# Four low parts of split weights trade places between VectorE and the adding DMA

## The chip, the cores and the metric

The kernel runs on one core of one Trainium2 chip. The metric is the device time of one execution in microseconds (us), taken as the median of several executions. A core has TensorE (PE in the profile; PEld is its weight load), VectorE (DVE), ScalarE (ACT), GpSimd (POOL), SyncE (SP), and 16 DMA engines that every queue shares.

## The reference

One decoder layer on 256 tokens with a model width of 1024, in float32, batch 1 and depth 1. Per layer it computes:

```
h = rms_norm(x, norm1_g);  proj = h @ w_in            # 1024 x 2560
attn = block-sparse attention on 8 heads of 64 (256 tokens: one causal block)
conv = silu(layer_norm(causal depthwise conv, 31 taps, of GLU))
x = x + concat(attn, conv) @ w_out                    # 1024 x 1024
h = rms_norm(x, norm2_g)
y = x + (silu(h @ w_gate) * (h @ w_up)) @ w_down      # 1024 x 2816, twice, and 2816 x 1024
```

The change touches only how the weights of the last line are prepared.

## The kernel before

**Two parts of every weight.** To keep float32 accuracy, the kernel splits each weight into a high part `wh` (the weight rounded to the form that TensorE multiplies fast) and a low part `wl` (the weight minus `wh`). Each product is then two or three matmuls: `wh` and `wl` against the activation, and `wh` against the activation's own low part. Weights are handled in pieces of 128 x 1024, numbered from 0. A high part is always made by ScalarE (line 278). A low part is made in one of two ways, in `low_part`:

- by VectorE: one subtraction, line 226;
- by adding DMA: ScalarE writes -`wh` into the place of `wl` (line 223), and a DMA that GpSimd issues adds the weight to it while it moves it (line 224). The weight comes from device memory for most pieces ("wl<-w" in the profile), or from a tile on chip where the piece is not stored as such ("wl<-t").

The list `BY_DMA` (line 65) names the pieces of the second kind.

**The order.** Nothing schedules at run time: the Python program writes the instructions of all engines in one fixed order, and every engine works through its own list in that order. Before each group of matmuls, `feed` (line 274) makes the high parts of the pieces up to some pieces ahead, and the low parts of those that are nearly due. `BEHIND` lists pieces whose high part is made some places earlier than their number says. Eight places hold pieces; a new piece takes the place of the lowest numbered one and so waits until TensorE is through with that.

**The stages around the change.** Pieces 28 to 71 are the gate and up weights: the loop over `f` from 0 to 21 (the lines of `mm2`, 307 and 309, tiles `fg` and `fu`) uses piece 28 + 2f for the gate and 29 + 2f for the up half, 16 pairs of matmuls in each `f`. After each `f`, `glu_task` evacuates the two banks with ScalarE (`gs`, `us`, line 314) and VectorE (`tg`, `ps`, `ac`, lines 315, 857, 871) and a Silu on ScalarE (line 859). Pieces 72 to 102 are the down projection, 11 pairs of weight blocks (line 953, tile `sum`). Nine of the pairs are "FAST": a Strassen-like scheme that forms seven products from sums of weight blocks. For such a pair VectorE makes the sums (`add_up`, lines 241 to 243, tile `t`), and the pair has three pieces: the first is the block as stored, the second and third are sums in `t`. Piece 72, 73 and 74 are those of pair 0, and 75, 76, 77 those of pair 1. Beside these three each FAST pair has a single block (`b11` or `other`, lines 207 and 208). At the end VectorE, and ScalarE with GpSimd, add the seven sums onto the residual (lines 1003 to 1020), and SyncE writes the result out.

Of the kernel before, what the change touches and what calls it, by code (L numbers as in the profile page):

```python
# [61 lines left out]
PLAIN = [p for p in range(NF // 2) if PAIRS[p] == "P"]  # L62
DOWN = 72
BEHIND = {75: 70, 78: 72, 81: 75, 82: 78, 83: 78, 86: 80, 89: 83, 92: 86, 95: 89, 98: 92}
BY_DMA = [*range(45, 64, 3), 73, 74, *BEHIND]
FAR = 46
SUMS = {66: 0, 69: 1}
FORMS_LATE = 11
# [72 lines left out]
def _build(nc, tc, t, ctx):  # L141
# [78 lines left out]
    def low_part(dst, src, by_dma=False):  # L220

        if by_dma:
            nc.scalar.activation(dst[1], dst[0].bitcast(F32), AF.Copy, scale=-1.0)  # L223
            nc.gpsimd.dma_start(dst[1], src.bitcast(F32R), accum_op=ALU.add)  # L224
        else:
            nc.vector.tensor_tensor(dst[1], src, dst[0].bitcast(F32), op=ALU.subtract)  # L226
# [27 lines left out]
    def home(j):  # L254

        i, a = divmod(j * PIECE, BW)
        if j >= DOWN:
            p, a = down[j - DOWN]
            if a and p in FAST:
                return None  # L260
            i, a = DOWN // 2 + p, (a if p in PLAIN else 1) * PIECE
        return t["w"][i - 2][:, a:a + PIECE]
# [11 lines left out]
    def feed(upto, more=1):  # L274
        last = DOWN + len(down) - 1
        while len(pieces) <= min(upto + more, last):
            dst, src, j = new_piece()
            nc.scalar.activation(dst[0], src, AF.Copy)  # L278
            if j in BY_DMA:
                low_part(dst, home(j) or src, True)  # L280
            waiting.append((dst, src, j))
            waiting.sort(key=lambda w: w[2])
        while waiting and waiting[0][2] <= upto:
            dst, src, j = waiting.pop(0)
            if j not in BY_DMA:
                low_part(dst, src)
# [802 lines left out]
```

## Time and profile before

| what | value |
|---|---|
| median of 3 runs | 286.4 us (286.2 to 286.47) |
| the profiled execution's own time | 287.12 us |
| its span, first to last instruction | 285.3 us |
| TensorE clock granted in it | 0.999 |
| PE busy | 279.6 us |
| DVE busy | 238.9 us |
| ACT busy | 207.2 us |
| POOL busy | 46.9 us |
| DMA moved | 69.03 MB |

The span lies 1.8 us under the profiled execution's own time, and that execution 0.7 us above the median of the runs; sums in the prediction are made against the profiled execution. An instruction's row in a timeline reads: start, duration, engine, line, operation, tile written <- tiles read, shapes, count, and in brackets how long its engine sat idle before it and what ended that. The printed end of one instruction may lie some 0.1 us behind the start of the next on the same engine, since they are pipelined. Share of busy time over the whole span is an average over stages; the tables by stage show what each stage is limited by.

### The profile page before, as it was taken

How to read it: one execution, taken by the hardware profiler on the slowest of the kernel's cores; microseconds unless marked ns; L12 is line 12 of the kernel's file. 1: busy time of each engine (PE TensorE's matmuls, PEld its weight loads, DVE VectorE, ACT ScalarE, POOL GpSimd, SP SyncE). 2: the span in 40 equal slices, each digit the busy share in tenths (PEclk: the TensorE clock that was granted, in tenths of full speed). 3: DMA queues.
4: the chain of work that ended last, by engine and by line, in shares of the span. 5: the costliest groups of instructions: out<-in, count | busy, mean ns of one | idle time of the engine just before them, and what ended most of it. 6: DMA issues, size and time to landing. Idle time of an engine off the chain costs nothing.

```text
span 285.3 us, 4176 instructions
## 1 busy us (share of the span) xinstructions
PE 279.6 (98%) x1463; PEld 234.1 (82%) x1463; DVE 238.9 (84%) x425; ACT 207.2 (73%) x336; POOL 46.9 (16%) x75
## 2 busy tenths in 40 slices
PE   8899999999999999999999999999999999999994
PEld 6688887778788888888888888888888878888883
DVE  3979996896894959999967687698789789999995
ACT  4858578986728677467878777776679799887480
POOL 0003555533000000000111111000012221211033
PEclk9999999999999999999999999999999999999999
DMA  7999958854203882849689998984676999999603
GB/s 228 409 423 341 420 188 275 314 177 177 119 0 148 319 308 110 295 149 369 229 273 289 300 324 227 288 273 167 231 223 153 247 270 255 316 318 194 170 14 147
DMA packets 13638, 69.03 MB, mean 242 GB/s; under 512 B 1777, under 2 KB 2385, under 8 KB 7730
## 3 DMA queue, kind: packets, MB, share of 16 engines
q1 hardware_dynamic: 10162, 56.19, 53.5%
q0 software_dynamic: 3312, 12.58, 21.5%
q8 instruction: 11, 0.18, 0.2%
q14 instruction: 9, 0.07, 0.1%
q10 hardware_dynamic: 144, 0.00, 0.0%
HBM read 65.62 MB, written 2.10 MB: 237 GB/s over the span
## 4 chain that ended last, share of the span: by engine, by line
PE 87%; DMA 6%; DVE 4%; issue 1%; POOL 0%; SPq 0%; ACT 0%; POOLq 0%
PE p L724 19%; PE sum L953 17%; PE fg L307 12%; PE fu L307 12%; PE po L770 8%; PE fg L309 6%; PE fu L309 6%; DMA wl<-t 4%; DMA first<-first 2%; PE S L558 1%; PE pT L588 1%; DVE wl L226 1%; PE O L744 1%; PE xT L786 1%; PE cv L318 0%
## 5 line engine op out<-in xcount | busy, mean ns | idle before, releaser
L278 ACT ACTIVATE wh<-raw 128x1024 fp32r<-128x1024 f32 x81 | 83.9, 1054 | 15.4 <-PE fu L307 7.5
L226 DVE TENSOR_TENSOR wl<-raw,wh 128x1024 fp32r<-128x1024 f32 x64 | 77.1, 1219 | 3.4 <-ACT wh L278 3.4
L307 PE MATMUL fu<-g,wh 128*128 128x512 f32 x176 | 62.5, 395 | 0.0
L307 PE MATMUL fg<-g,wh 128*128 128x512 f32 x176 | 62.4, 394 | 0.0
L309 PE MATMUL fg<-g,wl 128*128 128x256 f32 x176 | 48.8, 277 | 0.0
L309 PE MATMUL fu<-g,wl 128*128 128x256 f32 x176 | 48.8, 277 | 0.0
L307 PEld LDWEIGHTS fg<-g,wh 128*128 128x128 f32 x176 | 33.0, 187 | 7.7 <-DVE g L794 0.2
L307 PEld LDWEIGHTS fu<-g,wh 128*128 128x128 f32 x176 | 33.0, 188 | 7.6
L224 POOL DMA_DIRECT2D wl<-w x17 | 14.9, 877 | 133.2 <-ACT wl L223 61.8
L309 PEld LDWEIGHTS fg<-g,wl 128*128 128x128 f32 x176 | 33.1, 188 | 0.0
L309 PEld LDWEIGHTS fu<-g,wl 128*128 128x128 f32 x176 | 33.1, 188 | 0.0
L953 PE MATMUL sum<-wh,forms 128*128 128x512 f32 x96 | 29.5, 389 | 0.0
L724 PE MATMUL p<-wh,xh 128*128 128x512 f32 x80 | 25.9, 405 | 0.8 <-ACT wh L385 0.8
L278 ACT ACTIVATE wh<-t 128x1024 fp32r<-128x1024 f32 x18 | 19.1, 1059 | 8.0 <-DVE t L241 4.9
L724 PE MATMUL p<-wh,xl 128*128 128x512 f32 x80 | 24.8, 391 | 0.0
L724 PE MATMUL p<-wl,xh 128*128 128x512 f32 x80 | 24.7, 390 | 0.0
L953 PEld LDWEIGHTS sum<-wh,forms 128*128 128x128 f32 x96 | 18.0, 188 | 3.7
L223 ACT ACTIVATE wl<-wh 128x1024 fp32r<-128x1024 f32 x19 | 20.2, 1062 | 0.6
L226 DVE TENSOR_TENSOR wl<-t,wh 128x1024 fp32r<-128x1024 f32 x16 | 19.6, 1223 | 1.2 <-ACT wh L278 0.8
L953 PE MATMUL sum<-wl,forms 128*128 128x512 f32 x48 | 18.8, 391 | 0.3 <-DMA wl<-t 0.3
L724 PEld LDWEIGHTS p<-wh,xh 128*128 128x128 f32 x80 | 14.2, 189 | 5.3 <-ACT wh L385 1.6
L724 PEld LDWEIGHTS p<-wh,xl 128*128 128x128 f32 x80 | 15.0, 188 | 3.3
(208 smaller groups left out, 476.6 us busy)
## 6 DMA issues: line engine op xcount, KB each, us to landing
raw<-w SPq DMA_DIRECT2D x44, 1024.0 KB, 6.6
wl<-w POOLq DMA_DIRECT2D x17, 512.0 KB, 9.3
first<-first SPq DMA_DIRECT2D x8, 384.0 KB, 7.0
raw<-w SPq DMA_DIRECT2D x2, 512.0 KB, 7.5
xtok<-xtok SPq DMA_DIRECT2D x2, 512.0 KB, 8.8
x<-xtok SPq DMA_DIRECT2D x2, 512.0 KB, 6.7
kept<-x POOLq DMA_DIRECT2D x1, 1024.0 KB, 4.1
wl<-t POOLq DMA_DIRECT2D x2, 512.0 KB, 9.5
```

What stands on the lines that cost most here:

```text
L223: nc.scalar.activation(dst[1], dst[0].bitcast(F32), AF.Copy, scale=-1.0)
L224: nc.gpsimd.dma_start(dst[1], src.bitcast(F32R), accum_op=ALU.add)
L226: nc.vector.tensor_tensor(dst[1], src, dst[0].bitcast(F32), op=ALU.subtract)
L278: nc.scalar.activation(dst[0], src, AF.Copy)
L307: nc.tensor.matmul(out.rearrange("p (a q) -> p a q", a=2), w[0], both, start=z in first and z not in seen, stop=False)
L309: nc.tensor.matmul(out[:, 0:T], w[1], both[:, 0, :], start=False, stop=z in last and left[z] == 0)
L558: nc.tensor.matmul(banks[a][:, out], G["qT"][rows, j, q], G["kT"][rows, j, k], start=True, stop=True)
L588: nc.tensor.transpose(b[:, a * P:(a + 1) * P], p[:, a * P:(a + 1) * P], ident)
L724: nc.tensor.matmul(banks[i], (xh, xh, xl)[a][:, kt, sls[i]], w[a % 2], start=kt == 0 and a == 0, stop=kt == KT - 1 and a == 1)
L744: nc.tensor.matmul(o, vs[:, 0, hs], G["pT"][h][:, 0:T], start=True, stop=False)
L770: nc.tensor.matmul(po[i, n], G["mix"][l][:, k, i * P:(i + 1) * P], w[r], start=k == a == 0, stop=k == KT - 1 and a == 2)
L953: nc.tensor.matmul(banks[m], lhs, rhs, start=first, stop=last)
```

## The change

```diff
-BY_DMA = [*range(45, 64, 3), 73, 74, *BEHIND]
+BY_DMA = [*range(45, 72, 3), *BEHIND]
```

Before, the list held 45, 48, ... 63, then 73 and 74, and the ten of `BEHIND`. Now it holds 45, 48, ... 63, 66, 69 and the ten of `BEHIND`. So the low parts of pieces 66 and 69 (the gate weights of f = 19 and the up weights of f = 20) go from VectorE to the adding DMA, and those of 73 and 74 (the two sums of pair 0 of the down projection) from the adding DMA to VectorE. Instructions stay the same in number on every engine; no matmul changes. The order in which high parts are made, and the places that they take, stay as they are.

GpSimd's queue, where the adding DMAs are issued, as a difference (- before, + now):

```order
 L224 DMA wl60_1951<-w 128x1024
 L224 DMA wl63_2040<-w 128x1024
-L224 DMA wl75_2273<-w 128x1024
-L224 DMA wl78_2366<-w 128x1024
-L224 DMA wl73_2398<-t0_2340 128x1024
-L224 DMA wl74_2424<-t0_2340 128x1024
+L224 DMA wl66_2128<-w 128x1024
+L224 DMA wl69_2219<-w 128x1024
+L224 DMA wl75_2275<-w 128x1024
+L224 DMA wl78_2368<-w 128x1024
 L224 DMA wl81_2456<-w 128x1024
 L224 DMA wl82_2541<-w 128x1024
```

The two from the tile `t0` behind piece 78 are gone; two from device memory stand ahead of piece 75.

VectorE's list at the end of the gate and up loop (f = 19 and 20), where pair 0 and pair 1 of the down projection are prepared. Before:

```order
L208 TENSOR_TENSOR b11l_1081<-raw36_2072,b11h_1080 128x512
L315 TENSOR_TENSOR ps8_2344<-fu19_2334,us19_2403 128x256
L871 TENSOR_TENSOR ps8_2344<-ps8_2344,tg19_2370 128x256
L241 TENSOR_TENSOR t1_2428<-raw37_2131 128x1024
L242 TENSOR_TENSOR t1_2428<-t1_2428,raw37_2131 128x512
L243 TENSOR_TENSOR t1_2428<-t1_2428,raw37_2131 128x512
L315 TENSOR_TENSOR tg20_2432<-fg20_2395,gs20_2433 128x256
```

The same place now:

```order
L208 TENSOR_TENSOR b11l_1081<-raw36_2072,b11h_1080 128x512
L226 TENSOR_TENSOR wl73_2400<-t0_2342,wh73_2399 128x1024
L315 TENSOR_TENSOR ps8_2346<-fu19_2336,us19_2404 128x256
L871 TENSOR_TENSOR ps8_2346<-ps8_2346,tg19_2372 128x256
L226 TENSOR_TENSOR wl74_2425<-t0_2342,wh74_2424 128x1024
L241 TENSOR_TENSOR t1_2428<-raw37_2133 128x1024
L242 TENSOR_TENSOR t1_2428<-t1_2428,raw37_2133 128x512
L243 TENSOR_TENSOR t1_2428<-t1_2428,raw37_2133 128x512
L315 TENSOR_TENSOR tg20_2432<-fg20_2397,gs20_2433 128x256
```

Two subtractions of 128 x 1024 stand ahead of the sums `t1` of pair 1 and ahead of the evacuation of f = 20.

ScalarE's list at the same place. Before:

```order
L207 ACTIVATE b11h_1080<-raw36_2072 128x512
L278 ACTIVATE wh73_2397<-t0_2340 128x1024
L223 ACTIVATE wl73_2398<-wh73_2397 128x1024
L859 ACTIVATE tg19_2370<-tg19_2370 128x256
L314 ACTIVATE us19_2403<-fu19_2334 128x256
L278 ACTIVATE wh74_2423<-t0_2340 128x1024
L223 ACTIVATE wl74_2424<-wh74_2423 128x1024
L314 ACTIVATE gs20_2433<-fg20_2395 128x256
```

The same place now:

```order
L207 ACTIVATE b11h_1080<-raw36_2072 128x512
L278 ACTIVATE wh73_2399<-t0_2342 128x1024
L859 ACTIVATE tg19_2372<-tg19_2372 128x256
L314 ACTIVATE us19_2404<-fu19_2336 128x256
L278 ACTIVATE wh74_2424<-t0_2342 128x1024
L314 ACTIVATE gs20_2433<-fg20_2397 128x256
L278 ACTIVATE wh81_2455<-raw39_2249 128x1024
L223 ACTIVATE wl81_2456<-wh81_2455 128x1024
L859 ACTIVATE tg20_2432<-tg20_2432 128x256
L314 ACTIVATE us20_2462<-fu20_2398 128x256
L278 ACTIVATE wh76_2482<-t1_2428 128x1024
```

The two copies of line 223 are gone here, and stand directly behind `wh66` and `wh69`, earlier in the loop over `f`. What follows on ScalarE (`wh81`, `wl81`, the Silu of `tg20`, `us20`, `wh76`) is the same in both.

## The prediction

> **What bounds the kernel now.** I read the page first, then who keeps TensorE waiting, then busy time by stage, then the timelines of VectorE and ScalarE where the edit acts.
>
> ```profile
> span 285.3 us, 4176 instructions
> PE 279.6 (98%) x1463; PEld 234.1 (82%) x1463; DVE 238.9 (84%) x425; ACT 207.2 (73%) x336; POOL 46.9 (16%) x75
> ```
>
> Over the whole span TensorE looks like the only bound. Its waits, with the chain of waits around the one that touches the edit:
>
> ```profile
> PE sum L953 <- DMA wl<-t: 0.3, 1, 0.3
> 231.26 0.50 PE L953 MATMUL sum<-wl,forms 128*128 128x512 f32 x1 [0.29 <-DMA wl<-t]
> 221.17 10.05 DMA wl<-t
> 231.26 48.80 PE sum L953 x214
> ```
>
> The one stall behind the start is 0.29 us, at the first use of `wl74`, the second transfer of the kind that the change removes. Nothing more than that can be won on TensorE here. But the average hides a stage:
>
> ```profile
> core 0: us, PE busy (x) PEld busy (x) DVE busy (x) ACT busy (x) POOL busy (x), PEclk, DMA share, GB/s
> 217.00:227.00 10.00, 10.00 (x60) 8.74 (x59) 8.11 (x16) 8.42 (x14) 2.63 (x3) 1.00 0.99 220
> 227.00:240.00 13.00, 12.71 (x57) 10.20 (x56) 11.23 (x18) 12.60 (x18) 2.63 (x3) 1.00 1.03 247
> 240.00:250.00 10.00, 10.00 (x46) 8.27 (x45) 9.81 (x12) 8.59 (x9) 1.75 (x2) 1.00 1.04 319
> 250.00:260.00 10.00, 10.00 (x46) 8.29 (x45) 9.76 (x12) 8.40 (x10) 1.75 (x2) 1.00 1.05 290
> 260.00:270.00 10.00, 10.00 (x46) 8.29 (x45) 9.79 (x11) 5.42 (x7) 0.88 (x1) 1.00 0.76 156
> ```
>
> From 240 us on VectorE is as full as TensorE: 9.8 of 10 us in each stretch, the rest being gaps of hundredths between dependent steps. Who ends last is seen at the very end:
>
> ```profile
> 273.13 2.35 DVE L226 TENSOR_TENSOR wl<-raw,wh 128x1024 fp32r<-128x1024 f32 x2
> 275.41 0.69 DVE L1018 TENSOR_TENSOR rest<-sum,rest 128x512 f32<-128x512 f32 x1
> 276.75 4.31 DVE L1003 SCALAR_TENSOR_TENSOR raw<-sum,rstd,raw 128x512 f32<-128x512 f32 x6
> 280.97 0.47 DVE L1003 SCALAR_TENSOR_TENSOR raw<-sumleft,rstd,raw 128x256 f32<-128x256 f32 x1
> 281.53 0.48 DVE L1003 SCALAR_TENSOR_TENSOR raw<-sumright,rstd,raw 128x256 f32<-128x256 f32 x1
> 277.00 3.81 POOL L1008 TENSOR_TENSOR raw<-raw,rest 128x512 f32<-128x512 f32 x3 [0.36 <-ACT rest L1007]
> 276.96 0.39 PE L953 MATMUL sum<-wl,act 128*128 128x512 f32 x1
> ```
>
> VectorE runs back to back from its last low part (275.48) to 281.44, and the last addition, at 281.53, waits for TensorE. So VectorE reaches the end 0.09 us, or with the 0.08 us by which its instructions overlap 0.17 us, ahead of TensorE. **The kernel is bound by both**, and VectorE has 0.17 us to spare. GpSimd's three additions hang on VectorE's L1018 through ScalarE, so they give no slack of their own.
>
> The Trainium skill (Perfetto Trace Analysis, Identifying the Most-Contended Engine) takes the engine of the highest occupancy for the bottleneck. By that, work put on VectorE at 84% of the span would cost nothing, and the time would follow TensorE's stall; that result is the first rival. The same page says under Optimization Strategy that the most-contended engine may change over time; the stretches from 240 us agree, with VectorE at 98% there.
>
> **The change part by part.**
>
> *Low parts 66 and 69 by adding DMA.* ScalarE gains two copies of 1.06 us, at 192.0 and 200.4, right behind the high parts:
>
> ```profile
> 190.98 1.06 ACT L278 ACTIVATE wh<-raw 128x1024 fp32r<-128x1024 f32 x1 [0.64 <-PE fg L307]
> 193.76 1.06 ACT L278 ACTIVATE wh<-raw 128x1024 fp32r<-128x1024 f32 x1 [1.44 <-PE fu L307]
> 199.30 1.06 ACT L278 ACTIVATE wh<-raw 128x1024 fp32r<-128x1024 f32 x1 [0.51 <-PE fu L307]
> 202.08 1.06 ACT L278 ACTIVATE wh<-raw 128x1024 fp32r<-128x1024 f32 x1 [0.92 <-PE fg L307]
> 207.61 0.42 DVE L315 TENSOR_TENSOR ps<-fu,us 128x256 f32<-128x256 f32 x1 [2.15 <-PE fg L307]
> DMA to landing us min/median/max: 5.5/9.3/11.7
> 224.18 0.40 PE L307 MATMUL fu<-g,wh 128*128 128x512 f32 x1
> 224.53 0.39 PE L307 MATMUL fu<-g,wh 128*128 128x512 f32 x1
> ```
>
> The first copy fits into 1.44 us of idle time, the second overfills 0.92 by 0.1 us, which the next idle time takes. The transfers start near 193 and 201.5; at the slowest landing of any adding DMA (11.7) they are there by 205 and 213. The two matmul rows open the up half of f = 21: a pair takes 0.35 us, an `f` of 16 pairs 5.55, so the up half of f = 20 starts at 218.63 and f = 19 near 210.3: over 5 us to spare each. Cost nothing, hidden by that; a late transfer would cost its lateness. VectorE loses 2 x 1.14 us there and wins nothing, since at 207.61 it waits 2.15 us for f = 17 anyway.
>
> *Low parts 73 and 74 by VectorE.* The wait of 0.29 us on TensorE goes, and VectorE gets two subtractions in front of its full stretch. What they displace:
>
> ```profile
> 217.84 0.68 DVE L208 TENSOR_TENSOR b11l<-raw,b11h 128x512 fp32r<-128x512 f32 x1
> 218.82 0.42 DVE L315 TENSOR_TENSOR ps<-fu,us 128x256 f32<-128x256 f32 x1 [0.30 <-ACT us L314]
> 219.62 1.22 DVE L241 TENSOR_TENSOR t<-raw 128x1024 f32<-128x1024 f32 x1
> 222.66 0.42 DVE L857 TENSOR_TENSOR tg<-tg,r_bc 128x256 f32<-128x256 f32 x1
> 224.25 0.42 DVE L315 TENSOR_TENSOR ac<-fu,us 128x256 f32<-128x256 f32 x1 [1.17 <-PE fg L307]
> 225.36 1.22 DVE L226 TENSOR_TENSOR wl<-t,wh 128x1024 fp32r<-128x1024 f32 x1 [0.22 <-ACT wh L278]
> 226.50 0.42 DVE L878 TENSOR_TENSOR act<-ac,act 128x256 fp32r<-128x256 f32 x1
> 232.62 1.22 DVE L241 TENSOR_TENSOR t<-raw 128x1024 f32<-128x1024 f32 x1
> 239.04 0.69 DVE L208 TENSOR_TENSOR b11l<-raw,b11h 128x512 fp32r<-128x512 f32 x1 [0.34 <-ACT b11h L207]
> 222.58 1.06 ACT L223 ACTIVATE wl<-wh 128x1024 fp32r<-128x1024 f32 x1
> 223.55 0.40 ACT L859 ACTIVATE tg<-tg 128x256 f32<-128x256 f32 x1
> 224.26 1.06 ACT L278 ACTIVATE wh<-t 128x1024 fp32r<-128x1024 f32 x1
> ```
>
> An independent 1024-wide subtraction holds VectorE for 1.14 us (225.36 to 226.50); an engine starts 0.04 us after the end of what it waits for (`wh76`, 224.26 + 1.06, and 225.36). With these steps:
>
> - `wl73` starts at 218.44, the 0.68 of L208 less the overlap of 0.08 behind 217.84, and ends its hold at 219.58, where the evacuation `ps` starts (218.82 before: 0.76 late; the idle 0.30 us is used up). `wl74` starts at 220.38, once `ps` and L871 are through (`wh74`, which waits for TensorE to leave the gate of f = 20 at 218.63, is there by 219.8). The sums of pair 1 start at 221.52 instead of 219.62: 1.90 late, and L857 ends at 224.98 instead of 223.08.
> - Now ScalarE waits. Its Silu of `tg20`, behind `wl81` (over at 223.55), starts at 225.02 instead of 223.55; it and `us20` hold ScalarE 0.60 us, then `wh76` starts at 225.62 instead of 224.26, when TensorE's place let it: 1.36 late. The two copies that ScalarE lost gain nothing, for it waits for this.
> - VectorE's `ac` waits for `us20`: 225.73 (1.48 late; 0.42 of its idle 1.17 is taken up). `wl76` waits for `wh76`: 226.72, 1.36 late. From here each engine waits for the other through f = 21, so their idle times go with the lateness rather than soaking it up: the Silu of `tg21` 1.37 late, `wh77` 1.36, the sums of pair 2 at 233.99 instead of 232.62, `b11l` at 240.36 instead of 239.04, 1.32 late.
> - Behind that VectorE has no idle time left, so 1.32 us reach the tail.
>
> *Next late.* TensorE, 0.29 us earlier now, needs the last low part at 276.67 and gets it at 275.48 + 1.32 + 0.04 = 276.84: it stalls about 0.17 us, most of the gain. Then VectorE's own chain decides: 1.32 late less 0.17 to spare.
>
> *Sum.* 0 (66, 69) - 0 (TensorE's stall, not at the end any more) + 1.32 - 0.17 = **+1.15 us** on 287.12, so 288.27 for the profiled execution, and from the median of 286.4, 287.55. I say 287.5. No operation in this sum is without a row, so the bounds come from the lateness: none of it reaches the tail, and the stall of 0.29 is won (-0.29), or all of 2 x 1.14 = 2.28 does, less 0.17 (+2.11). I take the middle value since each of its steps is set by a row, and the same steps with the old list give back the old starts to 0.05 us.
>
> **The rivals.**
>
> 1. *TensorE alone decides.* The 2.28 us on VectorE are soaked up and the stall at `wl74` goes: 286.4 - 0.3 = 286.1. For it: by the stretches above VectorE idles 1.89 us from 217 to 227 and 1.77 to 240, more than 2.28 in all. Against it: each of these waits ends on ScalarE, which itself waits for VectorE. It holds if less than 0.17 us is left at 240; that makes it no change, and not slower.
> 2. *All of it arrives.* If ScalarE's later `wh` of pair 2 push VectorE once more, up to 2.28 us come through and TensorE stalls at each last low part: 286.4 + 2.1 = 288.5. Against it: ScalarE has two copies less to do in this stage.
> 3. *Transfers come late.* The two new ones, or block loads beside them, miss their use. The DMA engines have room there:
>
> ```profile
> 194.00:198.00 4.00, 4.00 (x25) 3.52 (x24) 3.08 (x7) 2.86 (x6) 0.00 (x0) 1.00 0.62 254
> ```
>
>    `wl66` would need over 17 us to land against the 11.7 seen; each us past that adds one to the forecast, 288.5 at 18 us.
> 4. *The relief helps.* The two transfers gone at 218 leave a share of 0.99 to 1.03 lighter, so loads land earlier. But no engine waits for a load there, so at best rival 1.
>
> **How the numbers follow.** Forecast 0.78, rival 1 with 4 0.13, rival 2 0.07, rival 3 0.02. The forecast's own range is 287.1 to 288.0 (lateness 0.9 to 1.8). A range of 8 in 10 that leaves out most of rivals 1 and 2: 286.6 to 288.1. A measurement of this kernel tells about 0.2%, 0.57 us, from no change: slower 0.82 (forecast, 2, 3, and less a small part of the forecast that falls under 287.0), same 0.14, faster 0.04, since no row offers more than 0.3 us.
>
> **What would show it.** Right: `wl73` and `wl74` on VectorE near 218.4 and 220.4; the idle time before `ac` of f = 20 shrunk from 1.17 to some 0.7; sums of pair 2 near 234; L1018 near 276.7; TensorE's wait on "wl<-t" gone and a short one on VectorE's `wl` near 276.7; the last addition waiting for VectorE itself or GpSimd, not TensorE. Wrong: VectorE's sums of pair 2 at 232.6 (rival 1); a TensorE wait on DMA near 210 or 218 (rival 3); L1018 past 277.3 (rival 2).

## The result, and the profile after

The changed kernel takes 288.07 us (median of 6 runs, 287.83 to 288.88) against 286.44 us for the kernel before on the same chip (6 runs, 286.20 to 287.01). The ratio is 1.0057, with a 95% interval of 1.0047 to 1.0067: **slower by 1.63 us** (1.35 to 1.92). Its profiled execution took 288.44 us.

The head of its page, and its chain of waits by engine:

```profile
span 286.3 us, 4175 instructions
PE 280.5 (98%) x1463; PEld 235.5 (82%) x1463; DVE 239.0 (83%) x425; ACT 207.3 (72%) x336; POOL 46.8 (16%) x75
PE 82%; DVE 9%; ACT 3%; issue 3%; POOL 0%; DVEq 0%; ACTq 0%
```

The same chain in the kernel before:

```profile
PE 87%; DMA 6%; DVE 4%; issue 1%; POOL 0%; SPq 0%; ACT 0%; POOLq 0%
```

Busy time has hardly changed on any engine (VectorE 238.9 before, 239.0 now). What has changed is the chain. The share of DMA is gone, that of TensorE has fallen, and VectorE's has doubled. The chain of the changed kernel in the down projection (start, duration, what), its beginning, a piece from the middle and one near the end, shows where:

```profile
226.86 9.57 PE sum L953 x42
...
239.54 0.53 ACT b11h L207
240.09 0.69 DVE b11l L208
240.78 1.07 DVE other L894 x2
241.85 1.15 DVE t L241
...
275.32 1.22 DVE wl L226
276.54 0.61 DVE rest L1018
```

Behind 236.43 us TensorE is not in it any more: VectorE and ScalarE take turns, and at the end GpSimd has a piece. Before, one row of TensorE, "231.26 48.80 PE sum L953 x214", reached from 231.26 to 280.06.

Busy time by stage of the changed kernel, at the edit and in the first full stretch behind it:

```profile
core 0: us, PE busy (x) PEld busy (x) DVE busy (x) ACT busy (x) POOL busy (x), PEclk, DMA share, GB/s
217.00:227.00 10.00, 10.00 (x60) 8.81 (x59) 8.98 (x15) 6.41 (x12) 0.88 (x1) 1.00 0.70 178
240.00:250.00 10.00, 10.00 (x46) 8.29 (x45) 9.72 (x13) 8.73 (x11) 2.45 (x3) 1.00 1.04 317
```

Where the edit acts, from 217 to 227, VectorE has gone from 8.11 to 8.98 us, ScalarE from 8.42 to 6.41, and the DMA share from 0.99 to 0.70. VectorE had 1.89 us free there before, and 0.87 of them are used now, for 2.28 us of added work; the rest of the 2.28 shows as work that now stands behind 227. From 240 on it is as full as it was (9.72 us, before 9.81).

The two executions did not reach this place at the same moment. In what follows, a time marked **"after the mark"** counts from the first matmul of the down projection in the one profiled execution of each kernel. TensorE works without a gap up to there in both (10.00 us of 10 from 217 to 227), so the change does not delay it:

```profile
226.95 0.62 PE L953 MATMUL sum<-wh,forms 128*128 128x512 f32 x2
```

That is the kernel before; this is the changed one, 0.26 us earlier:

```profile
226.69 0.63 PE L953 MATMUL sum<-wh,forms 128*128 128x512 f32 x2
```

VectorE's timeline of the changed kernel at the edit:

```profile
218.18 1.22 DVE L226 TENSOR_TENSOR wl<-t,wh 128x1024 fp32r<-128x1024 f32 x1
219.32 0.41 DVE L315 TENSOR_TENSOR ps<-fu,us 128x256 f32<-128x256 f32 x1
...
220.11 1.22 DVE L226 TENSOR_TENSOR wl<-t,wh 128x1024 fp32r<-128x1024 f32 x1
221.24 1.22 DVE L241 TENSOR_TENSOR t<-raw 128x1024 f32<-128x1024 f32 x1
...
225.46 0.42 DVE L315 TENSOR_TENSOR ac<-fu,us 128x256 f32<-128x256 f32 x1 [0.76 <-ACT us L314]
...
233.68 1.22 DVE L241 TENSOR_TENSOR t<-raw 128x1024 f32<-128x1024 f32 x1
```

`wl73` and `wl74` are the first and third rows. The sums of pair 1 start at 221.24, 1.62 us later than before on the clock and 1.88 later when both are counted from the mark. Those of pair 2 (last row) start 6.99 us after the mark, before 5.67: **1.32 us late**. ScalarE's timeline of the changed kernel shows what handed the delay on:

```profile
224.74 0.42 ACT L859 ACTIVATE tg<-tg 128x256 f32<-128x256 f32 x1 [1.35 <-DVE tg L857]
```

The Silu of `tg20` now waits 1.35 us for VectorE. The end of the changed kernel:

```profile
276.45 0.69 DVE L1018 TENSOR_TENSOR rest<-sum,rest 128x512 f32<-128x512 f32 x1
280.99 0.28 PE L953 MATMUL sumright<-wl,act 128*128 128x256 f32 x1
282.01 0.48 DVE L1003 SCALAR_TENSOR_TENSOR raw<-sumleft,rstd,raw 128x256 f32<-128x256 f32 x1
282.40 0.48 DVE L1003 SCALAR_TENSOR_TENSOR raw<-sumright,rstd,raw 128x256 f32<-128x256 f32 x1
```

TensorE's last matmul starts at 280.99, 54.30 us after the mark (before 54.26), so its result has long been there when VectorE adds it at 282.40, 55.71 after the mark. Before, the last addition stood at 54.58 (281.53) and waited for TensorE. The last addition now follows VectorE's own list and not TensorE, 1.13 us later when counted from the mark.

### The profile page after: what moved, and what is told of

It reads as the page before. It is cut to its first block, busy times and chain, and to the rows that moved or that the text cites. A ratio compares the mean times of both kernels' runs of the same rounds, so it can differ in the third digit from the quotient of the medians.

```text
span 286.3 us, 4175 instructions
## 1 busy us (share of the span) xinstructions
PE 280.5 (98%) x1463; PEld 235.5 (82%) x1463; DVE 239.0 (83%) x425; ACT 207.3 (72%) x336; POOL 46.8 (16%) x75
## 4 chain that ended last, share of the span: by engine, by line
PE 82%; DVE 9%; ACT 3%; issue 3%; POOL 0%; DVEq 0%; ACTq 0%
PE p L724 20%; PE fg L307 14%; PE fu L307 14%; PE po L770 8%; PE fu L309 7%; PE fg L309 7%; PE sum L953 3%; ACT wh L278 3%; DVE t L241 2%; DVE t L243 1%; DVE t L242 1%; PE warm L369 1%; DVE wl L226 1%; PE S L558 1%; PE pT L588 1%
## 5 line engine op out<-in xcount | busy, mean ns | idle before, releaser
L226 DVE TENSOR_TENSOR wl<-raw,wh 128x1024 fp32r<-128x1024 f32 x62 | 74.7, 1219 | 3.4 <-ACT wh L278 3.4
L224 POOL DMA_DIRECT2D wl<-w x19 | 16.6, 876 | 138.3 <-ACT wl L223 50.7
L953 PE MATMUL sum<-wh,forms 128*128 128x512 f32 x96 | 29.6, 390 | 0.0
L226 DVE TENSOR_TENSOR wl<-t,wh 128x1024 fp32r<-128x1024 f32 x18 | 22.0, 1222 | 1.2 <-ACT wh L278 0.8
L953 PEld LDWEIGHTS sum<-wh,forms 128*128 128x128 f32 x96 | 18.0, 188 | 3.7
L953 PE MATMUL sum<-wl,forms 128*128 128x512 f32 x48 | 18.8, 392 | 0.0
L724 PEld LDWEIGHTS p<-wl,xh 128*128 128x128 f32 x80 | 15.2, 190 | 3.3
```

The costliest lines, as they stand in the source:

```text
L724: nc.tensor.matmul(banks[i], (xh, xh, xl)[a][:, kt, sls[i]], w[a % 2], start=kt == 0 and a == 0, stop=kt == KT - 1 and a == 1)
L953: nc.tensor.matmul(banks[m], lhs, rhs, start=first, stop=last)
```

## The experiments

All are one-core kernels. Each ratio is to the kernel before, run beside it on the same chip. Each edit is to the changed kernel, unless it says that it is to the kernel before.

### Which part of the change costs

Only 66 and 69 by adding DMA (73 and 74 stay with it too):

```diff
-BY_DMA = [*range(45, 72, 3), *BEHIND]
+BY_DMA = [*range(45, 72, 3), 73, 74, *BEHIND]
```

> Half of the change alone: low parts 66 and 69 by adding DMA, 73 and 74 stay with the adding DMA. Theory (all of the cost is VectorE's lateness from 73 and 74): 286.4, no change, the 0.29 us wait of TensorE on the transfer of 74 still there, VectorE's sums of pair 2 where they were before. Rival A (the two new transfers or ScalarE's two copies carry the part of the measured +1.63 us that the forecast's +1.15 lacks): some 286.9.

Measured: 286.73 us against 286.50, ratio 1.0002 (0.9986 to 1.0017). The two new transfers and ScalarE's two copies cost nothing that can be measured. The interval alone would still leave room for rival A's 0.4 us; the rows do not: the sums of pair 2 start 5.67 us after the mark, as before, and the last addition 54.63, against 54.58.

Only 73 and 74 by VectorE:

```diff
-BY_DMA = [*range(45, 72, 3), *BEHIND]
+BY_DMA = [*range(45, 64, 3), *BEHIND]
```

> The other half alone: low parts 73 and 74 by VectorE, 66 and 69 stay with VectorE. Theory: as the whole change, 288.0 (+1.5), VectorE's L1018 some 1.3 us later than before when both are set against the same matmul. Rival A: about 287.6, the forecast's +1.15 alone.

Measured: 288.29 us against 286.50, ratio 1.0052 (1.0034 to 1.0069). The whole loss is here. Its sums of pair 2 start 6.99 us after the mark, as in the changed kernel.

Only 73 by VectorE, then only 74:

```diff
-BY_DMA = [*range(45, 72, 3), *BEHIND]
+BY_DMA = [*range(45, 64, 3), 74, *BEHIND]
```

> Low part 73 alone by VectorE, 74 stays with the adding DMA, 66 and 69 with VectorE. Theory, by the same steps as the forecast: the sums of pair 1 start 0.76 us late, the Silu of f = 20 0.33, the high part of piece 76 only 0.2 us, since it waited for TensorE's place anyway; so 0.2 us of lateness reach the tail and the time is 286.4 to 286.6, within 0.2 us of before. Rival B (each subtraction costs its own 1.14 us less what idle time soaks up evenly): half of the whole, 287.2.

Measured: 286.82 us against 286.50, ratio 1.0005 (0.9991 to 1.0018).

```diff
-BY_DMA = [*range(45, 72, 3), *BEHIND]
+BY_DMA = [*range(45, 64, 3), 73, *BEHIND]
```

> Low part 74 alone by VectorE, 73 stays with the adding DMA. Theory: it waits for its high part (219.8), so the sums of pair 1 start 1.3 us late, the high part of piece 76 0.8 us; 0.8 of lateness reach the tail, and with 0.1 to 0.17 to spare the time is 287.1 (+0.65 to 0.7). Rival B: half of the whole, 287.2, the same as with 73 alone. The theory has 74 cost some 0.5 us more than 73, rival B the same.

Measured: 287.51 us against 286.50, ratio 1.0031 (1.0017 to 1.0045).

The two subtractions are alike, 1.14 us each, but they don't cost alike. VectorE's rows with only 73 there (mark at 226.60):

```profile
220.03 1.22 DVE L241 TENSOR_TENSOR t<-raw 128x1024 f32<-128x1024 f32 x1
...
232.46 1.22 DVE L241 TENSOR_TENSOR t<-raw 128x1024 f32<-128x1024 f32 x1
```

And with only 74 (mark at 226.27):

```profile
220.26 1.22 DVE L241 TENSOR_TENSOR t<-raw 128x1024 f32<-128x1024 f32 x1
...
232.70 1.22 DVE L241 TENSOR_TENSOR t<-raw 128x1024 f32<-128x1024 f32 x1
```

And the row of ScalarE's `wh76` in the same two kernels, with only 73 first:

```profile
224.11 1.05 ACT L278 ACTIVATE wh<-t 128x1024 fp32r<-128x1024 f32 x1
```

and with only 74:

```profile
224.35 1.05 ACT L278 ACTIVATE wh<-t 128x1024 fp32r<-128x1024 f32 x1
```

The lateness against the kernel before, at four places, in us after the mark:

| by VectorE | sums of pair 1 | `wh76` | sums of pair 2 | last addition | median, against before |
|---|---|---|---|---|---|
| only 73 | 0.76 | 0.20 | 0.19 | 0.01 | +0.3, not told from 0 |
| only 74 | 1.32 | 0.77 | 0.76 | 0.57 | +1.0 |
| both | 1.88 | 1.32 | 1.32 | 1.13 | +1.6 |

Each row loses some 0.56 us on the way to `wh76`, and by the rows of the kernel before this has two parts. There the Silu of `tg20` started at 223.55, behind `wl81` on ScalarE, 0.43 us after VectorE's L857 (over at 223.08) would have let it; and `wh76` then waited some 0.14 us more for its place on TensorE. A further 0.18 or 0.19 goes at the end, the slack that VectorE had. What is left arrives whole. The subtraction of 73 comes in at 0.76 instead of 1.14 since it fills the 0.30 us that VectorE idled in front of `ps`, and the 0.08 by which instructions overlap there where none waits; that of 74 alone comes in at 1.32, since it also starts 0.18 us late, waiting for `wh74`. So 73 alone is soaked up, and 74 is not. A rival that gives each of the two an equal share of the cost falls, and so does one that puts it on the transfers of 66 and 69.

### Is VectorE's full stretch what hands it to the end?

Three low parts of single blocks leave VectorE in the stretch where it is full (the output lacks those three products' low parts, as the expectation says), in the changed kernel and in the kernel before:

```diff
-        split(b11[q % 3], blocks[i][:, 0:W], nc.vector)
+        if q in (3, 4, 5):
+            nc.scalar.activation(b11[q % 3][0], blocks[i][:, 0:W], AF.Copy)
+        else:
+            split(b11[q % 3], blocks[i][:, 0:W], nc.vector)
```

> The changed kernel with three of VectorE's subtractions left out in its full stretch: the low parts of the single blocks of the 4th, 5th and 6th FAST pair (128x512, some 0.6 us of VectorE each); TensorE multiplies what stands in their places, so its work is the same and the output is not the reference's. Theory (VectorE's 1.3 us of lateness is carried by a stretch without idle time and is all of the cost): 1.8 us less in the stretch buys it back, 286.2 to 286.6, TensorE ends last again. Rival (the cost arises on TensorE or in the transfers before 240 us): 288.2 as the change.

Measured, in the changed kernel: 286.88 us against 286.72, ratio 1.0005 (0.9996 to 1.0013).

> The kernel before with the same three subtractions left out. Theory (both engines bound the kernel, VectorE with 0.1 to 0.17 us to spare): TensorE ends as before, 286.3 to 286.5, no change, and its 0.29 us wait on the transfer of 74 stays. If VectorE alone bounds the kernel before: 284.7.

Measured, in the kernel before: 286.43 us, ratio 0.9994 (0.9985 to 1.0004).

VectorE's rows of the changed kernel with less work (mark at 226.50; its lines from 270 on are 3 higher, so L1021 is L1018):

```profile
233.50 1.22 DVE L241 TENSOR_TENSOR t<-raw 128x1024 f32<-128x1024 f32 x1
240.34 1.21 DVE L897 TENSOR_TENSOR other<-ps,other 128x384 fp32r<-128x384 f32 x2 [0.75 <-ACT other L894]
274.94 0.68 DVE L1021 TENSOR_TENSOR rest<-sum,rest 128x512 f32<-128x512 f32 x1
```

The sums of pair 2 are as late as ever, 7.00 us after the mark, but L1018 stands at 48.44 instead of 49.76. Of the 1.8 us taken off (3 x 0.60), 1.32 arrive; some 0.4 go into the first wait, 0.75 us instead of 0.33. The cost is gone with the lateness still there, so the lateness costs only because no free time follows on VectorE. TensorE does not end last, as the expectation had it: without a stall its last matmul starts 53.68 us after the mark, and the last addition, at 54.39, still follows VectorE's own list. The same cut in the kernel before wins nothing that can be measured, and its row says why:

```profile
274.33 0.69 DVE L1021 TENSOR_TENSOR rest<-sum,rest 128x512 f32<-128x512 f32 x1 [0.68 <-PE sum L956]
```

There VectorE waits for TensorE. The kernel before is bound by both. One part of the expectation missed: the profile of this run has no wait of TensorE on the transfer of 74.

### Can the lateness be avoided with 73 and 74 still on VectorE?

The sums of pairs 0 and 1 are made earlier in the loop over `f`, in the changed kernel and in the kernel before:

```diff
-SUMS = {66: 0, 69: 1}
+SUMS = {64: 0, 66: 1}
```

> The changed kernel with VectorE's sums for pair 0 moved two pieces of the gate and up loop forward, into its idle 2.15 us before 207.6, and the sums for pair 1 three pieces forward, to where those of pair 0 stood. Nothing is left out. Theory: low parts 73 and 74 then stand where the sums of pair 1 did, 2.28 us in place of 2.58; the Silu of f = 20 starts at 223.55 again, behind ScalarE's own work, and the lateness at the sums of pair 2 is 0; TensorE has no wait on a transfer. So 286.2 to 286.5, 1.6 us under the change. Rival (two subtractions more on VectorE after 217 us cost their time wherever its other work stands): 287.5 or more.

Measured, in the changed kernel: 286.59 us against 286.72, ratio 0.9998 (0.9990 to 1.0007).

> The kernel before (73 and 74 by adding DMA) with the same move of the sums. Theory: from 217 us on VectorE has 2.6 us less, but the Silu of f = 20 is then held by ScalarE's own list and the high part of piece 76 by TensorE's place, so nothing comes earlier at 232 us: 286.4, no change, TensorE's wait on the transfer still there. If earlier sums help by themselves: under 286.2.

Measured, in the kernel before: 286.78 us, ratio 1.0002 (0.9993 to 1.0012).

VectorE's rows of the changed kernel with the sums moved (mark at 226.32):

```profile
204.74 1.22 DVE L241 TENSOR_TENSOR t<-raw 128x1024 f32<-128x1024 f32 x1
...
207.33 0.42 DVE L315 TENSOR_TENSOR ps<-fu,us 128x256 f32<-128x256 f32 x1
...
231.99 1.22 DVE L241 TENSOR_TENSOR t<-raw 128x1024 f32<-128x1024 f32 x1
```

The sums of pair 0 now fill the 2.15 us in front of `ps` at 207.6 that VectorE idled away before. Sums of pair 2 start 5.67 us after the mark, exactly as in the kernel before, and the cost is gone, with 73 and 74 still on VectorE. So it is not the subtractions but their place that costs. Nothing is won on top, though TensorE has no stall here and its last matmul starts 53.68 us after the mark: the last addition follows VectorE's own list, at 54.43. Both kernels with the sums moved stay within the measurement of the kernel before, and no version here beats it.

### GpSimd as a way out

The single low parts of the full stretch go to GpSimd, in the changed kernel and in the kernel before:

```diff
-        split(b11[q % 3], blocks[i][:, 0:W], nc.vector)
+        split(b11[q % 3], blocks[i][:, 0:W], nc.gpsimd if q in (3, 4, 5) else nc.vector)
```

> The changed kernel, with three of VectorE's subtractions in its full stretch (the low parts of the single blocks of the 4th, 5th and 6th FAST pair, 128x512, each holding VectorE about 0.6 us) made by GpSimd, which is idle there, at about 1.3 us each. Theory (VectorE's chain from 240 us on decides the end, 1.3 us late): the lateness is bought back, TensorE ends last again, 286.2 to 286.6. Rival A (transfers and copies): no change from after, 288.0. If GpSimd slows VectorE while both read, the gain shrinks.

Measured, in the changed kernel: 290.48 us against 286.67, ratio 1.0141 (1.0125 to 1.0156).

> The kernel before, with the same three subtractions on GpSimd. Theory: TensorE is then the only bound, VectorE's slack at the end grows from 0.1 to over 1.5 us and is worth nothing; TensorE still waits 0.3 us for the transfer of 74: 286.3 to 286.4, no change. If VectorE alone were the bound before: 284.8.

Measured, in the kernel before: 289.20 us, ratio 1.0090 (1.0076 to 1.0104). No rows of it are read: its profiled execution took 1596.52 us.

And 73 and 74 by GpSimd, with a new list `BY_POOL = [73, 74]` that `feed` hands to `low_part`:

```diff
-        if by_dma:
+        if by_pool:
+            nc.gpsimd.tensor_tensor(dst[1], src, dst[0].bitcast(F32), op=ALU.subtract)
+        elif by_dma:
```

> The changed kernel, with low parts 73 and 74 made by GpSimd instead of VectorE, 128x1024, some 2.6 us each (twice the 1.3 of its 128x512 additions), so done by 222.5 where TensorE needs them at 229.5 and 231. Theory: VectorE as early as before and TensorE's wait gone: 286.2 to 286.4, since VectorE's own end has only 0.1 to 0.17 us to give. If GpSimd's reads hold VectorE up for what they overlap: up to 287.5.

Measured: 290.42 us against 286.67, ratio 1.0135 (1.0121 to 1.0149).

All three are slower than expected, and the two that have rows show one reason. GpSimd's rows with 73 and 74 there (lines from 225 on are 3 higher than in the changed kernel, and L224 is the new subtraction; mark at 226.66):

```profile
216.91 2.40 POOL L224 TENSOR_TENSOR wl<-t,wh 128x1024 fp32r<-128x1024 f32 x1 [0.66 <-DVE ps L874]
221.34 3.29 POOL L224 TENSOR_TENSOR wl<-t,wh 128x1024 fp32r<-128x1024 f32 x1 [2.03 <-PE fu L312]
```

VectorE's rows beside them:

```profile
217.21 2.38 DVE L860 TENSOR_TENSOR tg<-tg,r_bc 128x256 f32<-128x256 f32 x1
221.15 1.22 DVE L244 TENSOR_TENSOR t<-raw 128x1024 f32<-128x1024 f32 x1
222.40 2.77 DVE L245 TENSOR_TENSOR t<-t,raw 128x512 f32<-128x512 f32 x1
...
235.67 1.22 DVE L244 TENSOR_TENSOR t<-raw 128x1024 f32<-128x1024 f32 x1
```

A product that takes 0.42 us elsewhere takes 2.38, and ends 0.28 us after GpSimd's subtraction; a sum of 0.69 takes 2.77 and ends 0.54 after it. So the subtractions cost VectorE its time from GpSimd as well: the sums of pair 2 (last row) start 9.01 us after the mark, 3.34 late. With the single low parts on GpSimd in the changed kernel it is the same. GpSimd's row there:

```profile
240.23 1.63 POOL L208 TENSOR_TENSOR b11l<-raw,b11h 128x512 fp32r<-128x512 f32 x1
```

and VectorE's beside it, 2.55 us for what takes 1.15 elsewhere:

```profile
240.34 2.55 DVE L894 TENSOR_TENSOR other<-ps,other 128x384 fp32r<-128x384 f32 x2 [0.75 <-ACT other L891]
```

These runs can't test the theory as they were meant to: they move the work to an engine that holds up the one it was taken from. One comparison among them holds all the same. With the same three blocks on GpSimd, the change costs 290.48 - 289.20 = 1.28 us, near the 1.3 us of lateness.

### The kernel before, again

The kernel before, unchanged, against itself:

> The kernel before, unchanged, as a yardstick for what lies outside the span: 1.82 us in the one profiled execution of before, 2.08 to 2.16 in the six of after. If that difference belongs to the change, these runs show 1.8; if it belongs to the executions, they scatter up to 2.1. Time 286.4, ratio 1.000 within 0.1%.

Measured: 286.78 us against 286.67, ratio 1.0004 (0.9995 to 1.0013). Its profile has the sums of pair 2 at 5.67 us after the mark and the last addition at 54.66, against 5.67 and 54.58 in the other profile of this kernel. A single difference of 0.1 us after the mark is therefore not read as an effect.

## Why the prediction was right, point by point

- **Sign and size.** Forecast 287.5 (286.6 to 288.1), measured 288.07: slower, as forecast, just inside the range and 0.07 above the likeliest case's own (to 288.0). The sum of 1.15 us stands against 1.63. That the measured time lies inside the range, by 0.03 us, is in part luck: some 0.45 us of the cost come from two terms that the sum does not have (below).
- **66 and 69 cost nothing.** Right. Alone they give ratio 1.0002. GpSimd issues them at 193.17 and 201.49 (forecast "near 193 and 201.5"), they land after 7.9 and 8.8 us, and nothing waits for them. The rival of late transfers falls.
- **Two subtractions ahead of the sums; each step.** Right to some hundredths, once the 0.26 us by which this execution is earlier are taken off the forecast's clock:

| step | forecast, less 0.26 | measured |
|---|---|---|
| `wl73` | 218.18 | 218.18 |
| `wl74` | 220.12 | 220.11 |
| sums of pair 1 | 221.26 | 221.24 |
| Silu of `tg20` | 224.76 | 224.74 |
| `ac` of f = 20 | 225.47 | 225.46 |
| idle time before `ac` | about 0.7 | 0.76 |
| sums of pair 2 | 233.73 | 233.68 |

- **From pair 2 to the tail.** Right: "1.32 us reach the tail", and L1018 is 1.30 late after the mark (49.76 against 48.46).
- **VectorE's 0.17 us to spare.** Right: 0.18 to 0.19 in the runs with 73, 74 and both, and the last addition 1.13 late where 1.15 was forecast.
- **Rival 1, TensorE alone.** Falls: the last addition stands 1.41 us behind TensorE's last matmul start (282.40 - 280.99), before 0.32 (281.53 - 281.21). The Trainium skill (Perfetto Trace Analysis, Identifying the Most-Contended Engine) takes the engine of the highest occupancy for the bottleneck, but does not hold the matmuls' share, which the prediction used, for a good measure of TensorE's headroom, and names among others that of the weight loads instead. Here the matmuls' share over the span puts TensorE ahead, 98% to 83%, and that of the weight loads puts the two level, 82% to 83%; the time follows VectorE. **Rival 4**, the relief, falls too: the DMA share went from 0.99 to 0.70, and only 73 and 74 on VectorE with no other transfer moved gives the same loss.
- **Rival 2, all 2.28 arrive.** Falls: 1.32 arrive.

What was mis-sized:

- **The stall at `wl74`**, put at 0.29 us from the number in brackets. By starts it is about twice that. The rows of the kernel before around it, which the prediction did not show in full:

```profile
230.36 0.61 PE L953 MATMUL sum<-wh,forms 128*128 128x512 f32 x2
231.26 0.50 PE L953 MATMUL sum<-wl,forms 128*128 128x512 f32 x1 [0.29 <-DMA wl<-t]
231.60 0.62 PE L953 MATMUL sum<-wh,forms 128*128 128x512 f32 x2
```

Matmuls start 0.227 us apart there, so the pair at 230.36 should give way at 230.81 and does at 231.26: 0.45 late. The next start follows 0.34 later instead of 0.227: another 0.11, 0.56 in all. It agrees with TensorE's last matmul start: 54.26 us after the mark with the stall, 53.68 to 53.71 in five runs without any. This did not touch the forecast, since TensorE does not decide the end.
- **TensorE's new stall**, put at 0.17 us at the last low part. There are several: the changed kernel has stretched matmuls at three low parts, 0.1 to 0.2 us late by their starts, of which these are the last two, and no listed wait:

```profile
273.04 0.50 PE L953 MATMUL sum<-wl,other 128*128 128x512 f32 x1
276.59 0.50 PE L953 MATMUL sum<-wl,act 128*128 128x512 f32 x1
```

So TensorE, relieved by 0.58, ends where it ended before (54.30 against 54.26). The prediction's mark "a short one on VectorE's `wl` near 276.7" came as a stretched matmul at 276.59, not as a wait.
- **Two small terms were missing.** From the last addition to the end of the span it is 3.90 us now (286.3 - 282.40), 3.77 before (285.3 - 281.53): the last two additions now come 0.39 us apart instead of 0.56, and SyncE, which takes 0.33 to 0.44 us to issue an output, is still at the one before when the last is ready: it issues that 0.12 us behind the addition's end (283.00 against 282.88), before 0.03 (282.04 against 282.01). And the time that the execution takes beside its span is 2.14 us (288.44 - 286.3), 1.82 before (287.12 - 285.3). With them the sum is 1.13 + 0.13 + 0.32 = 1.58, against 1.63 measured and 1.15 forecast. Most of the first is SyncE's; the cause of the second **stays open**.

## What to carry to other kernels

Where two engines reach the end within tenths of each other, look for the point from which the busier one of a stage has no free time left, and follow a delay step by step up to that point: what is left of it there is the price, and what the engine's free time adds up to over the stage does not tell it. Two equal pieces of work need not cost the same, nor do their costs add up: the waits on the way soak up a fixed 0.56 us of lateness here, once, so that 73 alone leaves 0.2 us, 74 alone 0.8, and both 1.3. Ask before moving work to another engine whether the same work fits a gap further ahead on its own; here that took the cost away where the way over GpSimd more than doubled it.

## What the runs showed of the hardware

- **GpSimd and VectorE block each other.** While GpSimd subtracts one tile on chip from another, VectorE's instruction with two such inputs stands still until GpSimd is through: 0.42 us became 2.38, 0.69 became 2.77, and two additions of 1.15 us together became 2.55. In the other direction GpSimd's second subtraction, issued 0.19 us into a VectorE instruction of 1.22 us, took 3.29 instead of 2.40. The Trainium skill (SBUF — State Buffer, Who interferes with whom) states that a VectorE instruction with two inputs in SBUF and a GpSimd instruction that reads SBUF exclude one another for the whole instruction, whichever comes second. The rows agree in both directions.
- **The number in brackets before a matmul understates a stall**, since the ends of matmuls are modelled: 0.29 us listed, 0.56 by starts, 0.58 by TensorE's end. A stall of about 0.1 us shows only as a matmul of 0.50 us among others of 0.39.
- **The transfer into `wl74` lands unevenly**: TensorE's wait for it, as listed, was 0.3 us in the profile of the kernel before, 0.4 in another of the same kernel, 0.9 in the kernel before with the sums moved, and none in it with less work on VectorE. The medians of these kernels cannot be told apart; in the profile with 0.9 the last addition stands at 55.21 after the mark against 54.58.
- **Time beside the span** was steady to about 0.1 us in nearly all executions of a kernel (one of the kernel before took 2.3) but differed between kernels by 0.3 us: 2.1 for the changed kernel, with only 73 and 74 moved, with less work and with GpSimd's 73 and 74; 1.8 for the kernel before and with only 66 and 69; 1.9 with only 73, only 74 and the changed kernel with moved sums or with single low parts on GpSimd. No row of a profile lies in it, and its cause was not found.
